# Depthwise-conv taps handed out ahead of the matmuls, and decay work moved later, in a two-layer GLA and conv decoder trunk

## The chip, the cores and the metric

The kernel runs on one core of one Trainium2 chip. The metric is the device time of one execution, in microseconds; lower is better. Three runs of the kernel before gave a median of 1651.48 us, from 1650.69 to 1652.75.

Names used here: PE is TensorE (matmuls), ACT is ScalarE, DVE is VectorE, POOL is GpSimd, SP issues the weight loads. Each engine works through its own queue in program order.

## The reference, cut to what matters

A decoder trunk of two layers. Each layer is a SwiGLU FFN at half weight, a mixer, and a second such FFN, each behind an RMS norm. Tokens: 16 meta tokens and a prompt of 256 (one sequence), and 8 running sequences of 8 new tokens; 336 columns in all, 320 where the meta tokens are no longer wanted. The mixer, where everything of this change lies:

```python
proj = x @ w_in            # q, k, v, g, a_lr, glu (a, ga), m_a, m_b
loga = log_sigmoid(a_lr @ w_decay_up + b_decay) / 16      # per key channel
# gated linear attention in chunks, b = cumsum(loga)
scores = tril((q * exp(b)) @ (k * exp(-b)).T);  o = scores @ v + (q * exp(b)) @ S
S      = exp(b_last) * S + (k * exp(b_last - b)).T @ v
u = a * sigmoid(ga)                                       # conv input
c = silu(rmsnorm(depthwise_conv31(cat(conv_buf, u)) + b_dw))
merged = sigmoid(m_a) * rmsnorm(o) * gla_norm * silu(g) + sigmoid(m_b) * (c @ w_pw)
return merged @ w_out, S, last 30 rows of u per sequence
```

## The kernel before, in words

Activations stand transposed: 128 channels on the partitions, tokens in the columns. All big products are made of three matmuls with fp32r operands (high part by high part, high by low, low by high): `mm3`, L234. A block of 128 output channels takes 8 such triples over the input channels, 24 matmuls.

**Weights.** A plan (`weight_plan`, L67) lists the weight pieces (320 to 512 KB each) in the order of use. SP loads a piece to `raw` (4 buffers), ACT casts it to the high part `wh` (L205), and DVE (FFN and output weights) or POOL (all mixer weights but the last) subtracts to get the remainder `wl` (L207). Taking a piece (`use`, L211) issues the split of the piece three further on.

**The mixer's order** (L343 to L807) is written out by hand; nothing is reordered by a scheduler. On PE: GLU blocks 0 to 2 (each a gate `pga` and a product `pa`; L498), three groups of the value projection `v` (`v_proj`, L474, 72 matmuls each; the first also carries the 16 low-rank decay columns `lr`), GLU blocks 3 to 7, four blocks of queries, four of keys, three gate blocks, and then 21 more gate blocks with the four attention heads spread among them, before the pointwise and output projections. Twice per kernel, once per layer.

**Ticks.** Behind each triple of a projection `tick()` (L228) runs: it takes the next entry of a list of `tasks`, if there is one, and then calls `fill()`. The decay chain is such a list (L535 to L542): low-rank product `decay_z`, absolute value, exponential, logarithm, minimum on DVE, split into `lah` (ACT) and `lal` (POOL), running sums by matmul (`decay_prompt`, `decay_tail`), each at a fixed tick counted from the start of the second value group (24 ticks per value group, 16 per GLU block). So are the heads' steps (L719 to L753): scores and states 21 to 23 ticks into the head before, outputs from tick 0 on; in the last head the rest of the conv is issued at tick 4 (`conv_flush`), its norm's matmul at tick 8.

**The conv.** `conv_gen` (L384) issues the 31 taps of a channel block on DVE, each as a pair (272 prompt columns into bank `acc`, 64 sample columns into `acs`; one bank each, so the next block waits until ACT has copied both out, L401 to L404). `fill()` (L223) decides when a pair is issued, with two clocks of its own: `clock["pe"]` gets n / 2.4 + 2.5 ns for a matmul of n columns (four times that for fp32), `clock["dve"]` n x 1.04 + 110 ns for a DVE instruction (n x 6.25 + 110 for a reciprocal). Both are set to 0 where a mixer begins. One pair may be issued per tick, if `clock["dve"] + 7000 < clock["pe"]`.

**PSUM banks** (`bank`, L161): tag `mm` has four, `aux` two, `cv` and `cs` one each. A new tile of a tag takes the bank of that tag that came free first. A GLU product is evicted by DVE (times `rstd`), and its gate then goes through a sigmoid on ACT; a value group is evicted by ACT alone (L480 to L482).

Of the kernel before, what the change touches and what calls it, by code (L numbers as in the profile page):

```python
# [9 lines left out]
F32 = mybir.dt.float32  # L10
# [19 lines left out]
HEADS = 4  # L30
DK = 128
DV = 256
# [85 lines left out]
def trunk_kernel(ctx, tc, wts, x_in, vecs, consts, masks, wdecay, cache, state,  # L118
                 y_out, sp_out, ss_out, u_out):
    nc = tc.nc  # L120
    PE, ACT, POOL, SP = nc.tensor, nc.scalar, nc.gpsimd, nc.sync
    clock = {"pe": 0.0, "dve": 0.0}
# [6 lines left out]
    def mm(out, a, b, start, stop):  # L129
        n = 1  # L130
        for x in b.shape[1:]:
            n *= x
        clock["pe"] += (n / 2.4 + 2.5) * (4 if b.dtype == F32 else 1)
        PE.matmul(out, a, b, start=start, stop=stop)  # L134
# [26 lines left out]
    def bank(name, tag="mm", bufs=4):  # L161
        return psum.tile([128, 512], F32, tag=tag, name=name, bufs=bufs)
# [4 lines left out]
    def grp(g):  # L167
        return slice(g * 128, (g + 1) * 128)
# [51 lines left out]
    tasks = []  # L220
    filler = [None]

    def fill():  # L223
        if filler[0] is not None and clock["dve"] + 7000.0 < clock["pe"]:
            if next(filler[0], 0) == 0:
                filler[0] = None

    def tick():  # L228
        task = tasks.pop(0) if tasks else None
        if task is not None:  # L230
            task()
        fill()
# [110 lines left out]
    def mixer(l, norm, next_block):  # L343
# [6 lines left out]
        gp = gl.enter_context(tc.tile_pool(name="gla", bufs=1, reuse_waits="tile"))  # L350
# [2 lines left out]
        lal = mp.tile([128, 3, 512], F32R, tag="sb", name="lal")  # L353
        qt = gp.tile([128, HEADS, T], F32, name="qt")
        kt = gp.tile([128, HEADS, TP], F32, name="kt")
        kuT = gp.tile([128, 4, HEADS * DK], F32, name="kuT")
        v = gp.tile([128, 3, HEADS * DV], F32, name="v")
        dec = gp.tile([128, HEADS, 2 * NCH + NS], F32, name="dec")
        rT = gp.tile([128, 3], F32, name="rT")
# [16 lines left out]
        ACT.copy(wds[0:64], wdec[0:64])  # L376
        ACT.copy(wdr[64:128], wdec[64:128])
        POOL.tensor_tensor(out=wds[64:128], in0=wdec[64:128], in1=wdr[64:128].bitcast(F32), op=ALU.subtract)
        POOL.memset(kuT[0:64, 3], 0.0)
        cnorm = Norm()  # L380

        ready = [0]
# [41 lines left out]
        def decay_z(g):  # L424
            pz[g] = bank("pz", *(("aux", 2) if g < 2 else ("mm", 4)))
            mm(pz[g], alr[:, grp(g)], wds, True, True)
            la[g] = kp.tile([128, 512], F32, tag="la", name="la", bufs=3)
            ACT.activation(la[g], pz[g], AF.Abs)
# [9 lines left out]
        def decay_min(g):  # L438
            DVE.scalar_tensor_tensor(out=la[g], in0=pz[g], scalar=0.0, in1=la[g], op0=ALU.min, op1=ALU.subtract)

        def decay_split(g):
            ACT.copy(lah[:, g], la[g])
            POOL.tensor_tensor(out=lal[:, g], in0=la[g], in1=lah[:, g].bitcast(F32), op=ALU.subtract)

        def cumulate(out, hd, g):
            hs = slice(hd * DK, (hd + 1) * DK)
            m = cum[:, 0:2 * CHUNK] if g < NCH else cum[:, 2 * CHUNK:N_CUM]
            mm(out, lah[:, g, hs], m, True, False)
            mm(out, lal[:, g, hs], m, False, True)

        def decay_prompt(hd):
            pb = bank("pb", "aux", 2)
            for g in range(NCH):
                cumulate(pb[:, 2 * g * CHUNK:2 * (g + 1) * CHUNK], hd, g)
            v4 = pb.rearrange("p (g x c) -> p g x c", g=NCH, x=2)
            for dst, x, sign in ((qt, 0, 1.0), (kt, 0, -1.0), (ku, 1, 1.0)):
                ACT.activation(dst[:, hd, 0:SEQ].rearrange("p (g c) -> p g c", g=NCH), v4[:, :, x], AF.Exp,
                               scale=sign / TAU)
            ACT.activation(dec[:, hd, 0:2 * NCH], pb[:, CHUNK - 1::CHUNK], AF.Exp, scale=1.0 / TAU)

        def decay_tail(h0):
            pb = bank("pbt", "aux", 2)
            for e in range(2):
                cumulate(pb[:, 2 * e * TAIL:2 * (e + 1) * TAIL], h0 + e, NCH)
            v4 = pb[:, 0:4 * TAIL].rearrange("p (h x c) -> p h x c", h=2, x=2)
            hh = slice(h0, h0 + 2)
            for dst, x, sign in ((qt, 0, 1.0), (kt, 0, -1.0), (ku, 1, 1.0)):
                ACT.activation(dst[:, hh, SEQ:T], v4[:, :, x], AF.Exp, scale=sign / TAU)
            ACT.activation(dec[:, hh, 2 * NCH:], v4[:, :, 0, LS - 1:NSAMP:LS], AF.Exp, scale=1.0 / TAU)
# [4 lines left out]
        def v_proj(i):  # L474
            nw = V_WIDTH[i]
            nv = nw - (RANK if i == 0 else 0)
            pv = [bank("pv") for _ in range(3)]

            def evict(g):
                if i == 0:  # L480
                    ACT.activation(lr[:, g], pv[g][:, nv:nw], AF.Identity, scale=rT[:, g:g + 1])
                ACT.activation(v[:, g, V_OFF[i]:V_OFF[i] + nv], pv[g][:, :nv], AF.Identity, scale=rT[:, g:g + 1])  # L482

            for c in range(4):
                wh, wl = W.use("v")
                for g in range(3):
                    for k in range(2):
                        kk = 2 * c + k
                        mm(pv[g][:, :nw], xh[:, kk, grp(g)], wh[:, k], kk == 0, False)
                        mm(pv[g][:, :nw], xl[:, kk, grp(g)], wh[:, k], False, False)  # L490
                        mm(pv[g][:, :nw], xh[:, kk, grp(g)], wl[:, k], False, kk == KB - 1)
                        tick()
                    if c == 3:
                        evict(g)
# [36 lines left out]
        for j in range(3):  # L531
            glu_block(j)
        rstd = shared["rstd"]
        v_proj(0)
        at = {0: decay_lr, 12: decay_alr, 32: decay_exp, 36: decay_ln, 102: decay_end}  # L535
        for g in range(3):
            at.update({26 + g: lambda g=g: decay_z(g), 40 + g: lambda g=g: decay_min(g),
                       46 + 3 * g: lambda g=g: decay_split(g)})
        for hd in range(HEADS):
            at[64 + 5 * hd] = lambda hd=hd: decay_prompt(hd)  # L540
        at.update({86: lambda: decay_tail(0), 94: lambda: decay_tail(2)})
        tasks.extend([at.get(k) for k in range(103)])  # L542
        v_proj(1)
        v_proj(2)
        for j in range(3, KB):
            glu_block(j)
# [9 lines left out]
        def transposes(hd):  # L556
            pt = bank("ptr", "aux", 2)
            for g in range(3):
                PE.transpose(pt[:, grp(g)], ku[:, hd, grp(g)], ident)
                clock["pe"] += 108.0  # L560
            hs = slice(hd * DK, (hd + 1) * DK)
            ACT.copy(kuT[:, 0:3, hs], pt[:, :384].rearrange("p (g d) -> p g d", g=3))
            ACT.copy(kuT[64:128, 3, hs], pt[64:128, grp(2)])

        for hd in range(HEADS):
            pk = bank("pk")
# [42 lines left out]
            DVE.copy_predicated(probs[hd % 2].rearrange("p g c -> p (g c)")[:, :n], msk[:, :n], ps[:, :n])  # L609

        def prompt_state(hd, st, part):
            ks = slice(hd * DK, (hd + 1) * DK)
            vs = slice(hd * DV, (hd + 1) * DV)
            pu = bank("upd", "aux", 2)
            if part == 0:
                sp = st["sp"] = hp.tile([128, 2 * NCH, DV], F32, tag="sp", name="sp", bufs=1)
                mm(pu[:, 0:DV], kuT[:, 3, ks], v[:, 2, vs], True, True)
                ACT.activation(sp[:, 0], pu[:, 0:DV], AF.Identity, scale=dec[:, hd, 1:2])
                return
            sp = st["sp"]  # L620
            for g in range(NCH):
                mm(pu[:, g * DV:(g + 1) * DV], kuT[:, g, ks], v[:, g, vs], True, True)
            for g in range(NCH):
                if g:
                    ACT.activation(sp[:, 2 * g], sp[:, 2 * g - 1], AF.Identity, scale=dec[:, hd, 2 * g + 1:2 * g + 2])
                DVE.scalar_tensor_tensor(out=sp[:, 2 * g + 1], in0=sp[:, 2 * g], scalar=dec[:, hd, 2 * g:2 * g + 1],
                                         in1=pu[:, g * DV:(g + 1) * DV], op0=ALU.mult, op1=ALU.add)
            SP.dma_start(sp_out[l, hd], sp[:, 2 * NCH - 1])
# [11 lines left out]

        def mask_ku(hd, st):
            km = st["km"] = hp.tile([64, NS, DK], F32, tag="km", name="km", bufs=1)
            src = kuT[0:64, 2, hd * DK:(hd + 1) * DK]
            POOL.tensor_tensor(out=km, in0=src.unsqueeze(1).to_broadcast([64, NS, DK]),
                               in1=seqm[0:64].unsqueeze(2).to_broadcast([64, NS, DK]), op=ALU.mult)

# [72 lines left out]
        hs = [{} for _ in range(HEADS)]  # L719

        def head_start(hd):
            st = hs[hd]
            return {0: lambda: (scores(hd, st), mask_ku(hd, st)), 1: lambda: prompt_state(hd, st, 0),
                    2: lambda: prompt_state(hd, st, 1)}
# [25 lines left out]
        at = head_start(0)  # L750
# [236 lines left out]
```

## Time and profile before

| | before |
|---|---|
| median of three runs | 1651.48 us (1650.69 to 1652.75) |
| profiled execution, its own time | 1651.98 us |
| its span, first to last instruction | 1650.2 us |
| PE busy | 1617.0 us, 98% |
| DVE busy | 1080.9 us, 66% |
| ACT busy | 734.8 us, 45% |
| POOL busy | 423.6 us, 26% |
| mean granted PE clock | 0.990 |
| HBM read | 230.08 MB, 149 GB/s with the writes |

The busy shares are means over stages; in the mixers (about 253 to 597 us and 1082 to 1406 us) DVE is much busier than 66%. A granted clock of 1 is 2.4 GHz, 0.5 is 1.2 GHz. In a row of the timeline the number in brackets is the time for which the engine had nothing to do just before, with the instruction that ended it. The wait on `acc` by ACT's copy, for example, is time in which DVE could not begin the next conv block.

### The profile page before, as it was taken

The numbers are of one execution on the slowest core, as the hardware profiler recorded it, in microseconds if no ns is written. First come the engines' busy times: TensorE is split into PE (matmuls) and PEld (weight loads), VectorE is DVE, ScalarE is ACT, GpSimd is POOL, SyncE is SP. The second block draws the span as 40 slices with busy tenths as digits, with TensorE's granted clock in tenths as the row PEclk, the third lists the DMA queues.
The fourth block names the chain that finished last, engine by engine and source line by source line (L and its number), as shares of the span: only waits on it lengthen the run. The fifth ranks groups of instructions, "written<-read, shape, count | busy, mean of one in ns | idle before, by whom it ended". The sixth has DMA issues, their size and how long they took to land.

```text
span 1650.2 us, 27122 instructions
## 1 busy us (share of the span) xinstructions
PE 1617.0 (98%) x10612; PEld 1596.8 (97%) x10612; DVE 1080.9 (66%) x2159; ACT 734.8 (45%) x1148; POOL 423.6 (26%) x284
## 2 busy tenths in 40 slices
PE   8999999999999999999999999999999999999997
PEld 7999999999988999999999999999999889999997
DVE  7666446899885466555456564459998865666643
ACT  5433434753445444333333333347644554433432
POOL 0000017675563410000000000076756652000000
PEclk9999999999988999999999999999999999999999
DMA  5654445464452545443445544453644544444352
GB/s 200 200 182 129 133 152 163 134 182 152 129 170 87 166 128 154 145 140 120 147 156 184 174 136 138 151 153 126 193 159 143 169 135 155 146 154 153 116 170 79
DMA packets 76592, 247.56 MB, mean 150 GB/s; under 512 B 8624, under 2 KB 10928, under 8 KB 76208
## 3 DMA queue, kind: packets, MB, share of 16 engines
q1 hardware_dynamic: 75888, 240.34, 46.6%
q10 hardware_dynamic: 576, 5.49, 0.9%
q8 instruction: 83, 1.36, 0.3%
q14 instruction: 45, 0.37, 0.1%
HBM read 230.08 MB, written 15.71 MB: 149 GB/s over the span
## 4 chain that ended last, share of the span: by engine, by line
PE 88%; DVE 6%; ACT 3%; issue 1%; POOL 1%; DMA 0%; SPq 0%; DVEq 0%; POOLq 0%; ACTq 0%
PE pd L134 19%; PE pg L134 19%; PE pu L134 19%; PE pgate L134 5%; PE pga L134 4%; PE pa L134 4%; PE po L134 4%; PE pw L134 3%; PE pv L134 3%; PE pk L134 2%; PE pq L134 2%; PE o L134 2%; DVE acc L112 1%; DVE cl L112 1%; ACT wh L205 1%
## 5 line engine op out<-in xcount | busy, mean ns | idle before, releaser
L112 DVE TENSOR_TENSOR wl<-raw,wh 128x1024 fp32r<-128x1024 f32 (+1 forms) x320 | 349.3, 1108 | 228.0 <-ACT wh L205 227.5
L205 ACT CAST wh<-raw 128x1024 fp32r<-128x1024 f32 (+3 forms) x456 | 428.0, 956 | 77.0 <-issue 27.3
L207 POOL TENSOR_TENSOR wl<-raw,wh 128x1024 fp32r<-128x1024 f32 (+2 forms) x136 | 307.9, 2279 | 141.5 <-ACT wh L205 135.8
L270 POOL TENSOR_TENSOR ssum<-ssum,sq 128x336 f32<-128x336 f32 (+1 forms) x63 | 56.7, 901 | 1018.5 <-ACT sq L269 1018.5
L112 DVE SCALAR_TENSOR_TENSOR acc<-u,vec,acc 128x272 f32<-128x272 f32 (+1 forms) x480 | 234.5, 489 | 0.0
L134 PE MATMUL pg<-xh,wh 128*128 128x336 f32 (+1 forms) x704 | 223.1, 317 | 7.1 <-ACT wh L205 7.1
L134 PE MATMUL pu<-xh,wh 128*128 128x336 f32 (+1 forms) x704 | 221.8, 315 | 0.0
L134 PE MATMUL pg<-xh,wl 128*128 128x336 f32 (+1 forms) x704 | 221.2, 314 | 0.3 <-DVE wl L112 0.3
L134 PE MATMUL pg<-xl,wh 128*128 128x336 f32 (+1 forms) x704 | 221.2, 314 | 0.0
L134 PE MATMUL pu<-xh,wl 128*128 128x336 f32 (+1 forms) x704 | 221.1, 314 | 0.0
L134 PE MATMUL pu<-xl,wh 128*128 128x336 f32 (+1 forms) x704 | 221.1, 314 | 0.0
L134 PE MATMUL pd<-act_hi,wh 128*128 128x336 f32 (+1 forms) x704 | 221.0, 314 | 0.0
L134 PE MATMUL pd<-act_hi,wl 128*128 128x336 f32 (+1 forms) x704 | 220.3, 313 | 0.0
L134 PE MATMUL pd<-act_lo,wh 128*128 128x336 f32 (+1 forms) x704 | 220.2, 313 | 0.0
L134 PEld LDWEIGHTS pg<-xh,wh 128*128 128x128 f32 x704 | 132.6, 188 | 7.4 <-ACT wh L205 7.1
L326 ACT CAST act_hi<-pu 128x336 fp32r<-128x336 f32 (+1 forms) x88 | 38.5, 437 | 217.9 <-DVE pu L112 217.9
L134 PE MATMUL pgate<-xh,wh 128*128 128x336 f32 (+1 forms) x384 | 135.4, 352 | 0.0
L112 DVE SCALAR_TENSOR_TENSOR acs<-u,vec,acs 128x64 f32<-128x64 f32 x480 | 134.7, 281 | 0.0
L134 PEld LDWEIGHTS pg<-xh,wl 128*128 128x128 f32 x704 | 132.5, 188 | 0.8 <-DVE wl L112 0.8
L134 PEld LDWEIGHTS pg<-xl,wh 128*128 128x128 f32 x704 | 132.6, 188 | 0.4
L134 PEld LDWEIGHTS pu<-xh,wh 128*128 128x128 f32 x704 | 132.5, 188 | 0.0
L134 PEld LDWEIGHTS pu<-xh,wl 128*128 128x128 f32 x704 | 132.5, 188 | 0.0
(201 smaller groups left out, 3286.9 us busy)
## 6 DMA issues: line engine op xcount, KB each, us to landing
raw<-in_wts SPq DMA_DIRECT2D x304, 512.0 KB, 3.7
raw<-in_wts SPq DMA_DIRECT2D x64, 384.0 KB, 3.5
raw<-in_wts SPq DMA_DIRECT2D x64, 320.0 KB, 3.0
s<-in_state SPq DMA_DIRECT2D x16, 512.0 KB, 4.5
out_ss<-s SPq DMA_DIRECT2D x16, 512.0 KB, 5.3
raw<-in_wts SPq DMA_DIRECT2D x16, 344.0 KB, 3.6
u<-in_cache ACTq DMA_DIRECT2D x2, 2424.0 KB, 11.7
out_u<-u SPq DMA_DIRECT2D x16, 303.0 KB, 4.7
```

Source lines behind the costliest of these rows:

```text
L112: return fn(*args, **kw)
L134: PE.matmul(out, a, b, start=start, stop=stop)
L205: ACT.copy(wh[:, :nk * nw], raw)
L207: eng.tensor_tensor(out=wl[:, :nk * nw], in0=raw, in1=wh[:, :nk * nw].bitcast(F32), op=ALU.subtract)
L270: eng.tensor_tensor(out=self.sum[:, 0:n], in0=self.sum[:, 0:n], in1=sq[:, 0:n], op=ALU.add)
L326: ACT.copy(ah[:, j, 0:n], pu[:, 0:n])
```

## The change

Three things. `fill()` first lifts DVE's clock to PE's, and then issues pairs in a loop until DVE's clock is 1000 ns ahead of PE's (it leaves the loop if the generator has nothing to issue). The decay tasks are put at later ticks: transposed low-rank columns from tick 12 to 20, `decay_z` from 26 to 44, exponential from 32 to 50, logarithm from 36 to 54, minimum from 40, 41, 42 to 63, 65, 67, splits from 46, 49, 52 to 66, 70, 74, the heads' running sums from 64, 69, 74, 79 to 82, 87, 92, 97, tails from 86 and 94 to 103 and 109, the end from 102 to 118; two of the three tiles of the first value group come from `aux` instead of `mm`. The transposed keys `kuT` are laid out by head, then by group, instead of by group, then by head.

```diff
@@ -221,9 +221,13 @@
     filler = [None]
 
     def fill():
-        if filler[0] is not None and clock["dve"] + 7000.0 < clock["pe"]:
+        clock["dve"] = max(clock["dve"], clock["pe"])
+        while filler[0] is not None and clock["dve"] < clock["pe"] + 1000.0:
+            before = clock["dve"]
             if next(filler[0], 0) == 0:
                 filler[0] = None
+            if clock["dve"] == before:
+                break
@@ -353,7 +357,7 @@
-        kuT = gp.tile([128, 4, HEADS * DK], F32, name="kuT")
+        kuT = gp.tile([128, HEADS, 4, DK], F32, name="kuT")
@@ -376,7 +380,7 @@
-        POOL.memset(kuT[0:64, 3], 0.0)
+        POOL.memset(kuT[0:64, :, 3], 0.0)
@@ -474,7 +478,7 @@
-            pv = [bank("pv") for _ in range(3)]
+            pv = [bank("pv", *(("aux", 2) if i == 0 and g < 2 else ("mm", 4))) for g in range(3)]
@@ -532,14 +536,14 @@
         v_proj(0)
-        at = {0: decay_lr, 12: decay_alr, 32: decay_exp, 36: decay_ln, 102: decay_end}
+        at = {0: decay_lr, 20: decay_alr, 50: decay_exp, 54: decay_ln, 118: decay_end}
         for g in range(3):
-            at.update({26 + g: lambda g=g: decay_z(g), 40 + g: lambda g=g: decay_min(g),
-                       46 + 3 * g: lambda g=g: decay_split(g)})
+            at.update({44 + g: lambda g=g: decay_z(g), 63 + 2 * g: lambda g=g: decay_min(g),
+                       66 + 4 * g: lambda g=g: decay_split(g)})
         for hd in range(HEADS):
-            at[64 + 5 * hd] = lambda hd=hd: decay_prompt(hd)
-        at.update({86: lambda: decay_tail(0), 94: lambda: decay_tail(2)})
-        tasks.extend([at.get(k) for k in range(103)])
+            at[82 + 5 * hd] = lambda hd=hd: decay_prompt(hd)
+        at.update({103: lambda: decay_tail(0), 109: lambda: decay_tail(2)})
+        tasks.extend([at.get(k) for k in range(119)])
@@ -558,9 +562,8 @@
-            hs = slice(hd * DK, (hd + 1) * DK)
-            ACT.copy(kuT[:, 0:3, hs], pt[:, :384].rearrange("p (g d) -> p g d", g=3))
-            ACT.copy(kuT[64:128, 3, hs], pt[64:128, grp(2)])
+            ACT.copy(kuT[:, hd, 0:3], pt[:, :384].rearrange("p (g d) -> p g d", g=3))
+            ACT.copy(kuT[64:128, hd, 3], pt[64:128, grp(2)])
@@ -609,17 +612,16 @@
-                mm(pu[:, 0:DV], kuT[:, 3, ks], v[:, 2, vs], True, True)
+                mm(pu[:, 0:DV], kuT[:, hd, 3], v[:, 2, vs], True, True)
...
-                mm(pu[:, g * DV:(g + 1) * DV], kuT[:, g, ks], v[:, g, vs], True, True)
+                mm(pu[:, g * DV:(g + 1) * DV], kuT[:, hd, g], v[:, g, vs], True, True)
@@ -640,7 +642,7 @@
-            src = kuT[0:64, 2, hd * DK:(hd + 1) * DK]
+            src = kuT[0:64, hd, 2]
```

## Rows read from the trace of the kernel before

**Rows 1.** The page, busy time of each engine (us, share, instructions).

```profile
PE 1617.0 (98%) x10612; PEld 1596.8 (97%) x10612; DVE 1080.9 (66%) x2159; ACT 734.8 (45%) x1148; POOL 423.6 (26%) x284
```

**Rows 2.** Waits of PE: us in total, how many, the longest.

```profile
PE pga L134 <- ACT v L482: 4.0, 2, 2.0
PE pgate L134 <- POOL wl L207: 3.9, 3, 1.6
PE pw L134 <- POOL wl L207: 3.3, 2, 1.7
PE nrm L134 <- POOL ssum L270: 3.2, 2, 2.2
```

**Rows 3.** Stretches of 5 us: busy time of each engine, granted clock, DMA.

```profile
490.00:495.00 5.00, 5.00 (x22) 5.00 (x22) 4.79 (x4) 2.44 (x3) 4.96 (x4) 0.50 0.18 28
...
1310.00:1315.00 5.00, 5.00 (x41) 4.96 (x40) 4.90 (x3) 4.09 (x5) 3.51 (x3) 1.00 0.22 88
```

**Rows 4.** Timeline of PE, conv norm and last head's norm: start, us, instruction, idle before.

```profile
487.09 1.49 PE L134 MATMUL nrm<-ssum,ones_d 128*128 128x336 f32 x2 [2.16 <-POOL ssum L270]
...
510.41 0.73 PE L134 MATMUL nrm<-ssum,ones_v 128*128 128x336 f32 x2
...
1309.40 0.81 PE L134 MATMUL nrm<-ssum,ones_d 128*128 128x320 f32 x2 [1.02 <-POOL ssum L270]
...
1323.05 0.70 PE L134 MATMUL nrm<-ssum,ones_v 128*128 128x320 f32 x2
```

**Rows 5.** Chain that ended last, in order of time: blocks of 24 matmuls.

```profile
266.01 3.68 PE pa L134 x24
...
314.53 5.50 PE pga L134 x24
...
1143.21 3.95 PE pga L134 x24
```

**Rows 6.** Timeline of ACT, first layer, 306 to 324 us.

```profile
306.27 1.67 ACT L432 ACTIVATE la<-la 128x512 f32<-128x512 f32 x3
...
308.90 1.28 ACT L436 ACT_TABLE_LOAD   x1
310.19 1.95 ACT L436 ACTIVATE la<-la,one 128x512 f32<-128x512 f32 x3
312.05 0.35 ACT L401 COPY u<-acc 128x256 f32<-128x256 f32 x1
...
321.67 0.45 ACT L515 ACTIVATE gate<-pga 128x336 f32<-128x336 f32 x1 [2.52 <-DVE pga L112]
322.02 1.99 ACT L205 CAST wh<-raw 128x1024 fp32r<-128x1024 f32 x2
```

**Rows 7.** Timeline of DVE: block 1's gate, and first taps of conv blocks 1 and 2.

```profile
266.22 0.51 DVE L112 TENSOR_TENSOR pga<-pga,rstd 128x336 f32<-128x336 f32 x1
...
288.84 0.56 DVE L112 TENSOR_SCALAR acc<-u,vec 128x272 f32<-128x272 f32 x1 [0.67 <-ACT u L404]
...
312.62 0.56 DVE L112 TENSOR_SCALAR acc<-u,vec 128x272 f32<-128x272 f32 x1 [4.97 <-ACT u L404]
...
1117.48 0.55 DVE L112 TENSOR_SCALAR acc<-u,vec 128x256 f32<-128x256 f32 x1 [0.25 <-ACT u L401]
...
1136.98 0.55 DVE L112 TENSOR_SCALAR acc<-u,vec 128x256 f32<-128x256 f32 x1 [1.21 <-ACT u L401]
```

**Rows 8.** Timeline of POOL, first layer: decay remainders and weight remainders.

```profile
320.06 2.56 POOL L443 TENSOR_TENSOR lal<-la,lah 128x512 fp32r<-128x512 f32 x2
323.14 4.77 POOL L207 TENSOR_TENSOR wl<-raw,wh 128x1024 fp32r<-128x1024 f32 x2 [0.53 <-ACT wh L205]
```

**Rows 9.** Timeline, first layer's last head: state, its use, last conv copy.

```profile
476.50 0.51 ACT L625 ACTIVATE sp<-sp,dec 128x256 f32<-128x256 f32 x1 [0.55 <-DVE sp L112]
...
478.07 0.39 PE L134 MATMUL o<-qt,sp 128*128 128x128 f32 x2
...
484.99 0.37 ACT L401 COPY u<-acc 128x256 f32<-128x256 f32 x1 [2.56 <-DVE acc L112]
```

More of the change, by code (lines that the diff above doesn't have):

```diff
@@ L611, in prompt_state @@
         def prompt_state(hd, st, part):
-            ks = slice(hd * DK, (hd + 1) * DK)
             vs = slice(hd * DV, (hd + 1) * DV)
```

## The prediction

> **What bounds the kernel now.** I read the busy shares first, then what PE (TensorE) waited for, then a table of stretches with the granted clock, then the two places that this shows, row by row. PE is busy for 98% of the span [rows 1], so time can come only from PE's idle gaps and from stretches in which its clock is halved. The list of PE's waits shows where the gaps are [rows 2]: 4.0 us in two pieces of 2.0, one in each layer, for ACT's (ScalarE's) evictions of `v`, 3.2 us for the sum of squares behind the conv norm, 7.2 us for weight remainders from POOL. The table of stretches shows the other loss: from 490 to 495 us, in the first layer, the granted clock is 0.50, that is 1.2 of 2.4 GHz, and in the same stage of the second layer it is 1.00 [rows 3]. So both layers do the same work, one with a slow clock: the second layer is the price list for the first.
>
> The slow stretch, row by row [rows 4]: in the first layer the conv norm's matmul waits 2.16 us (487.09), and up to the last head's norm (510.41) 23.32 us pass; in the second layer the wait is 1.02 us, and the same stretch takes 13.65 us (1309.40 to 1323.05). The difference is 9.67 us; some 45 matmuls there are 336 columns wide in one layer and 320 in the other, 0.3 us, so the half clock costs 9.3 us. The other place is the first gate of GLU block 3 [rows 5]: behind the wait of 2.0 us 24 matmuls take 5.50 us, in the second layer, behind the same wait, 3.95 us, and undisturbed (at 266.01) 3.68 us: another slow stretch, 5.50 - 3.95 = 1.55 us.
>
> **Why PE waits there.** GLU block 3: ACT is in order, and before it may evict the last group of `v` it has the exponentials, a table load of 1.28, the logarithms (1.95 us for three) and conv block 1's copies, which start at 312.05 [rows 6]. DVE (VectorE) meanwhile had finished conv block 1 at 312.62 - 4.97 = 307.65 and stands for those 4.97 us until the copies are done [rows 7]. Conv norm: the last conv block is copied out at 484.99 [rows 9], 2.1 us ahead of the matmul that waits for its squares. DVE has fallen behind because the planner keeps it 7 us back.
>
> **The change, part by part.** *Hand-out of taps.* By the planner's formulas a tap pair costs 393 + 177 = 570 ns, three matmuls 427.5 ns; on the chip the 31 pairs of conv block 1 take 18.81 us, 0.61 us each (288.84 to 307.65; 18.29 us and 0.59 in the second layer) [rows 7], and three matmuls 3.68 / 8 = 0.46 us [rows 5]. Both are 1.04 to 1.08 times the planner's, so the planner's lead or lag holds on the chip. After GLU block 0 the clocks stand at 48 x 0.1425 + 0.6 = 7.4 us (PE) and 2.3 + 1.6 = 3.9 us (DVE: reciprocals, products). Before, no pair is handed out until PE is 7 us ahead; after, DVE's clock is set to PE's and pairs are issued up to 1 us ahead. Carrying both clocks through the program gives the pairs that stand ahead of each eviction: block 1's gate 0 before and 8 after, block 2's second product 15 and 22, block 3's gate 73 and 83 (second layer 75 and 86), the last head's scores 235 and 240 (237 and 243), of 248. No DVE work is added or taken away; evictions get 4 to 6 us more of it in front of them. DVE reaches block 1's gate at 266.22 before [rows 7], and would at 266.22 + 8 x 0.61 = 271.1 after; PE is done with it at 266.01 [rows 5], so the lag is 5 us. Up to the end of conv block 1 DVE's queue holds the same work, so that it ends at 307.65 in both.
>
> *Other banks for the first value group.* PE ends GLU block 2 and begins the value projection at 266.01 + 3 x 3.68 = 277.05; with that lag block 2's last product leaves its bank at about 282. Two tiles in the `aux` banks and one in block 1's bank (free at about 272) are there in time and cost nothing; three tiles in `mm` would have made PE wait for it, some 3 us.
>
> *Exponentials behind the value projection.* Same instructions and as many table loads, 16 to 18 ticks later (the transposes 8). ACT now stands at conv block 1's copies until 307.65 (a wait hidden by weights that are split three pieces ahead), then does copies and square (about 1.0), three casts (1.0 each [rows 6]), and is at the evictions of `v` at about 311.7. PE ends the projection at 314.53 - 2.0 = 312.5. So the two waits of 2.0 us go, and with the first its slow stretch of 1.55: -5.6 us.
>
> What is late next: the running sums of the first head, at tick 82. PE reaches them 35 triples after 312.5, at 312.5 + 35 x 0.46 = 328.6. They need both remainders `lal` of groups 0 and 1, which POOL makes behind two weight remainders, the first of which needs a cast that ACT issues behind block 3's sigmoid. DVE comes to block 3's gate 21 pairs after 307.65: 307.65 + 0.4 + 21 x 0.61 = 320.9, done 321.3. ACT has, from 307.65, some 1.0 + 4 x 1.0 + 3.0 (three evictions and three absolute values, taken as the sigmoid's 0.45 to 0.5 each) + 1.28 + 1.67 + 1.28 + 1.95 = 14.2 us of work, to 321.9, then table load and sigmoid 1.73 [rows 6]. So the cast ends between 322.8 (DVE alone) and 324.6 (ACT in full). POOL then has 4.77 + 2.56 = 7.33 us [rows 8]: 330.1 to 331.9, against 328.6. A new wait of 1.5 to 3.3 us; I take 2.7, nearer to ACT's chain because ACT is in order. In the second layer DVE ends block 1 at 1136.98 - 1.21 = 1135.77 [rows 7], 24 pairs follow, and PE ends the projection at 1143.21 - 2.0 = 1141.2: the same sums give 2.1 and 2.7, and I take 2.4. Together +5.1 us. The clock fell after one of two waits of 2 us there; I count one slow stretch: +1.55 us.
>
> *The end of the conv.* At the last scores 5 pairs fewer are left (3.0 us), in the second layer 6 (3.5 us), while the waits were 2.16 and 1.02 us. DVE's lag at this point should be near that of before: its extra pairs (7 x 0.61 = 4.3 us) are paid by the 4.97 us in which it no longer stands, and PE is earlier by only 2.0 + 1.55 - 2.7 = 0.9 us. So both waits go, -3.2 us, and the clock stays up: -9.3 us. What comes late behind it is the weight remainders: with PE back at full clock POOL, ACT and DVE have 9.3 us less there to prepare them. The five such waits of both layers sum to 7.2 us, none over 1.7 [rows 2]; another one in the first layer costs 0 to 1.7, and I take 1.0, between the two.
>
> *Keys by head.* Same copies, same sizes; the waits list has no PE wait on `kuT` [rows 2]. POOL's memset has the same elements. Zero; no PE wait on the masked keys stands there either, so what POOL does with them has cover.
>
> **Sum**: -5.6 + 5.1 + 1.55 - 3.2 - 9.3 + 1.0 = -10.5 us against the profiled execution's 1651.98 us (span 1650.2): **1641.5 us**. That execution is 0.5 us over the median of three.
>
> **A rule against it.** In the rows the clock is halved right behind the wait of 2.16 us, and not behind one of 2.0 us in the second layer [rows 4, 5]. So a wait of this size is enough in one place and not in another, and whether it is the cause is a reading. The Trainium skill, page "TensorE: Matmul & The Clock Gate", section on HAM oscillation, warns only of longer idle gaps than these; by it the waits would not be the cause, the clock would fall all the same, and the sum would be 9.3 us higher. The first layer's trace speaks against it, the fall being at the wait itself.
>
> **Rivals.**
> - *No wait at tick 82*: ACT and POOL get through sooner than I add up, or the lag is smaller. For it: my chain adds seven durations, and 2 us off each would do. Against: DVE's path alone is late by 1.5. Time: 1641.5 - 5.1 - 1.55 = 1634.9.
> - *The clock falls in the first layer's head stage anyway*, with or without a wait: many short matmuls lie there, and a wait of 2.0 us did not halve the clock in the second layer [rows 5]. Against: the fall is right at the wait [rows 4], and the second layer's same stage keeps 1.00 [rows 3]. Time: 1641.5 + 9.3 = 1650.8, no change.
> - *Slower: the head stage waits for DVE.* The state `sp` is ready at 476.50 + 0.51 = 477.01 and used at 478.07 [rows 9]: 1.06 us of slack. If DVE's lag there grows by more (it would if its 4 us were not paid back, for example by new waits at ACT's copies), PE waits some 4.3 - 1.06 = 3.3 us in each layer and the clock halves in both: 1641.5 + 6.6 + 2 x 9.3 = 1667. Against: the payback above; it decides from a lag of 1.1 us more than before.
>
> **Chances.** Forecast 0.52 (1640 to 1647: no or both slow stretches, waits of 1.5 to 3.3 us, a remainder of the conv wait); no wait 0.26; clock falls anyway 0.11; slower 0.11. Three runs of before spread over 2 us, so 0.2% (3.3 us) is about what can be told from no change. Faster 0.78, same 0.11, slower 0.11. The range takes in the first two cases with their bounds, from 1633 to 1648; the other two, 0.22, are left out but for their near edge.
>
> **What would show it.** Right: no PE wait on `v` at GLU block 3; a wait of PE on POOL's `lal` or on weight remainders in GLU block 5; no wait of the norm on `ssum`; clock 1.00 in the stretch that was at 0.50; DVE without its 4.97 us. Wrong: a PE wait on ACT's `sp` or on `probs`, a granted clock under 0.9 in either head stage, or GLU evictions that hold a bank so long that PE waits for DVE.

## The result, and the profile after

The changed kernel took 1641.28 us, the median of four executions (1639.13 to 1642.78), against 1651.15 for the kernel before beside it: a ratio of 0.9945, interval [0.9929, 0.9961], 0.55% faster. The forecast was 1641.5. The profiled execution took 1640.1 us (span 1638.3, mean granted clock 0.997). Ratios and ranges in this document compare fast executions only and leave out two that were far off, one of 6316.68 us of the kernel before and one of 2166.25 us (mean clock 0.747) of the last variant below.

The page after, busy time of each engine, answers to [rows 1]: DVE, ACT and POOL do the same work, PE is busy for 8.6 us less.

```profile
PE 1608.4 (98%) x10612; PEld 1588.8 (97%) x10612; DVE 1081.3 (66%) x2159; ACT 732.8 (45%) x1148; POOL 422.8 (26%) x284
```

What PE waited for after (us in total, how many, the longest), to be laid beside [rows 2]; a wait of 6.8 us for the first weights, 7.1 before, is not shown:

```profile
PE pgate L134 <- POOL wl L207: 4.3, 4, 1.6
PE pb L134 <- POOL lal L447: 3.4, 4, 1.3
PE pw L134 <- POOL wl L207: 3.3, 2, 1.7
PE upds L134 <- DVE s L112: 1.0, 1, 1.0
...
PE nrm L134 <- POOL ssum L274: 0.2, 1, 0.2
```

The two waits on `v` are gone, the conv norm's 3.2 us are 0.2, the late remainders cost 7.6 instead of 7.2, and there are new waits: 3.4 us on `lal`, and one of 1.0 us for DVE's update of the sample states `s`.

The clock after, stretches of 5 us (busy time of PE, PEld, DVE, ACT, POOL, granted clock, DMA share, GB/s): the first layer's last head runs at 1.00 where it ran at 0.50 [rows 3], and a short new loss stands in the second layer's head 1.

```profile
490.00:495.00 5.00, 5.00 (x31) 3.68 (x30) 4.96 (x10) 4.02 (x7) 1.61 (x3) 1.00 0.30 102
...
1255.00:1260.00 5.00, 3.95 (x20) 2.89 (x19) 5.00 (x13) 2.28 (x6) 2.74 (x5) 0.87 0.31 107
1260.00:1265.00 5.00, 5.00 (x27) 4.84 (x27) 3.22 (x11) 1.12 (x2) 5.00 (x4) 0.78 0.11 12
```

PE's timeline after: two of the sums' waits, the norms of [rows 4], and the new wait in head 1 of the second layer.

```profile
328.46 0.28 PE L134 MATMUL pb<-cum,lah 128*128 128x256 f32 x1
330.03 0.38 PE L134 MATMUL pb<-cum,lal 128*128 128x256 f32 x1 [1.29 <-POOL lal L447]
...
331.26 0.39 PE L134 MATMUL pb<-cum,lal 128*128 128x256 f32 x1 [0.72 <-POOL lal L447]
...
480.69 0.73 PE L134 MATMUL nrm<-ssum,ones_v 128*128 128x336 f32 x2
...
483.84 0.83 PE L134 MATMUL nrm<-ssum,ones_d 128*128 128x336 f32 x2 [0.15 <-POOL ssum L274]
...
497.06 0.73 PE L134 MATMUL nrm<-ssum,ones_v 128*128 128x336 f32 x2
...
1256.92 1.91 PE L134 MATMUL upds<-v,km 32*128 32x256 f32 x8 [0.96 <-DVE s L112]
...
1298.26 0.70 PE L134 MATMUL nrm<-ssum,ones_d 128*128 128x320 f32 x2
...
1311.15 0.70 PE L134 MATMUL nrm<-ssum,ones_v 128*128 128x320 f32 x2
```

These landmarks and those of [rows 4] split the gain by place. Up to the first layer's conv norm, 487.09 to 483.84: -3.25 us. From there to the last head's norm, 23.32 to 13.22 us: -10.10. From there to the second layer's conv norm the lead over the kernel before shrinks from 13.35 to 11.14 us: +2.21. Second layer, conv norm to last head's norm, 13.65 to 12.89: -0.76. Together -11.90, all of the difference of the spans (1650.2 to 1638.3).

The rows of the other engines after are to be laid beside [rows 6 to 9]. First ACT's timeline:

```profile
307.30 0.37 ACT L405 COPY u<-acc 128x256 f32<-128x256 f32 x1 [5.70 <-DVE acc L112]
...
313.42 0.57 ACT L486 ACTIVATE v<-pv,rT 128x344 f32<-128x344 f32 x1
...
322.49 0.45 ACT L519 ACTIVATE gate<-pga 128x336 f32<-128x336 f32 x1
322.84 1.99 ACT L205 CAST wh<-raw 128x1024 fp32r<-128x1024 f32 x2
...
480.37 0.38 ACT L405 COPY u<-acc 128x256 f32<-128x256 f32 x1
```

DVE's timeline, the gates of blocks 1 and 3 and the first tap of conv block 2:

```profile
271.15 0.51 DVE L112 TENSOR_TENSOR pga<-pga,rstd 128x336 f32<-128x336 f32 x1
...
307.90 0.56 DVE L112 TENSOR_SCALAR acc<-u,vec 128x272 f32<-128x272 f32 x1 [0.44 <-ACT u L408]
...
320.63 0.50 DVE L112 TENSOR_TENSOR pga<-pga,rstd 128x336 f32<-128x336 f32 x1
```

POOL's timeline, weight and decay remainders:

```profile
323.95 4.80 POOL L207 TENSOR_TENSOR wl<-raw,wh 128x1024 fp32r<-128x1024 f32 x2 [5.04 <-ACT wh L205]
328.72 2.49 POOL L447 TENSOR_TENSOR lal<-la,lah 128x512 fp32r<-128x512 f32 x2
```

DVE comes to block 1's gate at 271.15 (worked out: 271.1) and to block 3's at 320.63 (320.9), and its stand of 4.97 us is 0.44. ACT now waits ahead of conv block 1's copy, 5.70 us, and PE has no wait there.

### The profile page after: what moved, and what is told of

The parts are those of the page before. It is cut to its first block, busy times and chain, and to the rows that moved or that the text cites. A ratio compares the mean times of both kernels' runs of the same rounds, so it can differ in the third digit from the quotient of the medians.

```text
span 1638.3 us, 27112 instructions
## 1 busy us (share of the span) xinstructions
PE 1608.4 (98%) x10612; PEld 1588.8 (97%) x10612; DVE 1081.3 (66%) x2159; ACT 732.8 (45%) x1148; POOL 422.8 (26%) x284
## 4 chain that ended last, share of the span: by engine, by line
PE 85%; DVE 10%; ACT 2%; issue 1%; POOL 1%; DMA 0%; SPq 0%; DVEq 0%; POOLq 0%; ACTq 0%
PE pd L134 19%; PE pg L134 19%; PE pu L134 19%; PE pgate L134 6%; PE po L134 4%; PE pw L134 4%; DVE acc L112 3%; PE pa L134 2%; PE pga L134 2%; PE pk L134 2%; PE o L134 2%; PE pq L134 2%; PE pv L134 1%; DVE acs L112 1%; DVE cl L112 1%
## 5 line engine op out<-in xcount | busy, mean ns | idle before, releaser
L134 PEld LDWEIGHTS pu<-xl,wh 128*128 128x128 f32 x704 | 132.6, 188 | 0.0
```

## The experiments

Each time is the median of 5 to 12 executions. In its executions beside the first four runs the kernel before itself ranged from 1646.09 us (mean granted clock 0.994) to 1654.54 (0.988).

**Hand-out and banks alone.** The kernel before with the new `fill()`, and:

```diff
-            pv = [bank("pv") for _ in range(3)]
+            pv = [bank("pv", *(("aux", 2) if i == 0 and g < 2 else ("mm", 4))) for g in range(3)]
```

> The kernel before with the new hand-out of taps and the new banks of the first value group; the decay tasks stay at their old ticks, the keys in their old layout. Theory A (the gain comes from the decay tasks, because DVE no longer stands for 5 us at conv block 1 and so the conv ends sooner; the early hand-out only moves DVE work about): the two waits of PE on `v` stay, about 2 us each, DVE still stands for about 5 us behind conv block 1, the last conv copy comes within 1 us of 485.0, the conv norm still waits about 2 us in the first layer and its head stage runs at 0.50: 1651, within 2 us of the kernel before. Rival B (the hand-out ahead is what ends the conv sooner): the last conv copy 3 to 5 us earlier, no conv norm wait, clock 1.00 there: 1651.5 - 3.2 - 9.3 + 1 = 1640, with the `v` waits still in the list.

Measured: 1651.63 us, ratio 1.0016 [1.0004, 1.0028], no gain. But the place is the rival's: the conv norm waits 0.15 us, and the last head takes 13.21 us to its norm. The gain is given back at GLU block 3. PE's timeline of this run:

```profile
319.16 0.65 PE L134 MATMUL pga<-xh,wh 128*128 128x336 f32 x1 [5.29 <-DVE la L112]
...
1141.29 0.65 PE L134 MATMUL pga<-xh,wh 128*128 128x336 f32 x1 [5.86 <-ACT v L486]
```

ACT's timeline of it, conv block 1's copy and the exponentials:

```profile
308.64 0.37 ACT L405 COPY u<-acc 128x256 f32<-128x256 f32 x1 [3.93 <-DVE acc L112]
...
312.45 1.67 ACT L436 ACTIVATE la<-la 128x512 f32<-128x512 f32 x3
```

With taps handed out earlier, conv block 1's copies are issued ahead of the exponentials; ACT stands 3.93 us for DVE there, the exponentials start at 312.45 instead of 306.27 [rows 6], and the waits of 2.0 us become 5.3 and 5.9, with half clock behind them in both layers.

**Decay ticks alone.** The kernel before with this part of the diff alone:

```diff
-        at = {0: decay_lr, 12: decay_alr, 32: decay_exp, 36: decay_ln, 102: decay_end}
+        at = {0: decay_lr, 20: decay_alr, 50: decay_exp, 54: decay_ln, 118: decay_end}
...
-        tasks.extend([at.get(k) for k in range(103)])
+        tasks.extend([at.get(k) for k in range(119)])
```

> The kernel before with the new ticks of the decay tasks alone; hand-out of taps, banks and keys as before. Theory A: no wait of PE on `v`, DVE's stand behind conv block 1 under 1 us, last conv copy near 480.4, no conv norm wait over 0.5 us, first layer's head stage at 1.00. GLU evictions have 4 to 6 us less DVE work ahead of them than in the changed kernel, so the weight remainders and `lal` come earlier and the wait at the running sums is 0 to 3.4 us: 1638 to 1642. Rival B: the conv norm wait and the half clock stay, the `v` waits with their slow stretch go: 1651.5 - 5.6 + 0 to 3 = 1646 to 1649.

Measured: 1650.43 us, ratio 1.0003 [0.9990, 1.0015]. No wait on `v`, 0.44 us of stand behind conv block 1, `lal` 2.7 us: as theory A has it. But the conv norm waits as before. ACT's timeline of this run, the last conv copy:

```profile
483.44 0.37 ACT L401 COPY u<-acc 128x256 f32<-128x256 f32 x1 [2.56 <-DVE acc L112]
```

PE's timeline of it, third head's norm and the two conv norms:

```profile
480.38 0.73 PE L134 MATMUL nrm<-ssum,ones_v 128*128 128x336 f32 x2
...
485.54 0.86 PE L134 MATMUL nrm<-ssum,ones_d 128*128 128x336 f32 x2 [2.16 <-POOL ssum L270]
...
1304.83 0.90 PE L134 MATMUL nrm<-ssum,ones_d 128*128 128x320 f32 x2 [1.02 <-POOL ssum L270]
```

The last conv copy stands 3.06 us behind the third head's norm (483.44 - 480.38), exactly as before (484.99 - 481.93), although DVE no longer loses 4.97 us at conv block 1. DVE's timeline of this run shows most of that loss again, in GLU blocks 3 to 5:

```profile
322.68 0.64 DVE L112 TENSOR_TENSOR u<-pa,gate 128x16 f32<-128x16 f32 x3 [1.19 <-ACT gate L515]
...
333.70 0.52 DVE L112 TENSOR_TENSOR pga<-pga,rstd 128x336 f32<-128x336 f32 x1 [1.00 <-PE pga L134]
...
338.36 0.56 DVE L112 TENSOR_SCALAR acc<-u,vec 128x272 f32<-128x272 f32 x1 [3.55 <-ACT u L404]
```

The stand at conv block 2's copies was 0.44 us before (336.81). And in the heads DVE waits for PE in both kernels, so a lead from the GLU blocks is not carried through them: for `upds` between 400 us and the last conv copy 2.6 us before, 1.8 us here. After the change the copy stands 0.32 us ahead of the third head's norm (480.37 - 480.69). That is 3.4 us better, and the 5 pairs of 0.61 us that no longer stand between make up 3.05 of it. So neither part gains alone; together they gain 10 us.

**Only the last pairs moved.** The run above, with a smaller lag from the first head on:

```diff
-        if filler[0] is not None and clock["dve"] + 7000.0 < clock["pe"]:
+        if filler[0] is not None and clock["dve"] + lag[0] < clock["pe"]:
...
+        lag[0] = 4000.0
         at = head_start(0)
```

> The kernel before with the new decay ticks, the old banks and keys, and the old hand-out up to the first head; from there the lag that the planner keeps is 4000 ns instead of 7000. It asks which part of the new hand-out ends the conv norm's wait. Theory (it is the 5 or so pairs that no longer stand ahead of the last conv copy, wherever they were issued): by the planner 240 pairs stand ahead of the last scores (235 before, 240 in the changed kernel), the last conv copy comes right with the third head's norm instead of 3.06 us behind it, no wait on the sum of squares, granted clock 1.00 in the first layer's last head; no waits on `v`, `lal` 2.7 us as in the run with the new ticks alone: 1641.3 - 0.7 = 1640.6, or 1637.5 if the wait for DVE in the second layer's head 1 and its slow stretch also go. Rival (the lead has to be built up early, since DVE is behind by then): wait of about 2 us and half clock as with the ticks alone, 1650.

Measured: 1646.19 us, 1643.01 to 1657.84, ratio 0.9991 [0.9972, 1.0011]; the time of the theory, 1640.6, was missed. Most of its mechanism is there: 240 pairs ahead of the last scores, the last copy 0.37 us behind the third head's norm, no conv norm wait in the second layer, the last head at 1.00. Of the first layer's wait 0.84 us are left, PE's timeline:

```profile
487.36 0.83 PE L134 MATMUL nrm<-ssum,ones_d 128*128 128x336 f32 x2 [0.84 <-POOL ssum L271]
```

But DVE has the pairs to do in the heads now: PE waits 2.6 us for `s` instead of 1.0, and the clock falls behind two of these waits in the profiled execution (0.94 us at 444.02, 1.40 us at 1261.21). Four of the twelve executions took 1652.06 to 1657.84 us at a mean clock of 0.992 or less; none of these was profiled. Here a lead built up early did better than one built up in the heads.

**Conv norm later.** The kernel before with:

```diff
-                at.update({4: conv_flush, 8: conv_norm_a, 12: conv_norm_b, 23: lambda: head_norm_a(hd, st),
+                at.update({4: conv_flush, 12: conv_norm_a, 23: lambda: head_norm_a(hd, st),
...
-                    at[k] = lambda b=b: conv_scale(b)
+                    at[k] = lambda b=b: (conv_scale(b) if b else (conv_norm_b(), conv_scale(0)))
```

> The kernel before with the conv norm's matmul four ticks later (tick 12 instead of 8) and its inverse two ticks later, all else as before. It asks whether the wait makes the clock fall. Theory (the wait of 2.16 us is the cause): no wait of PE on the sum of squares in either layer, first layer's head stage at 1.00, 1651.5 - 3.2 - 9.3 + 0 to 2 (scales 2 ticks later, weight remainders) = 1639 to 1641. Rival (the clock falls there anyway): 0.50 in that stage all the same, 1651.5 - 3.2 = 1648.

Measured: 1647.72 us, ratio 0.9987 [0.9976, 0.9998]. No wait at the norm, yet the clock falls a little later in both layers, behind waits that were not there before (first layer) or were shorter (second layer, 0.37 us for `s`); PE's timeline:

```profile
493.08 1.97 PE L134 MATMUL upds<-v,km 32*128 32x256 f32 x6 [0.50 <-ACT sd L285]
...
1314.46 2.32 PE L134 MATMUL upds<-v,km 32*128 32x256 f32 x8 [1.65 <-DVE s L112]
```

By itself this run does not decide between the wait and "the clock falls anyway"; the time is the rival's.

**Conv norm earlier.** The changed kernel with the wait put back; run twice.

```diff
-                at.update({4: conv_flush, 8: conv_norm_a, 12: conv_norm_b, 23: lambda: head_norm_a(hd, st),
+                at.update({4: conv_flush, 6: conv_norm_a, 12: conv_norm_b, 23: lambda: head_norm_a(hd, st),
```

> The changed kernel with the conv norm's matmul two ticks earlier (6 instead of 8). It puts a wait of about 2 us back in the first layer's last head and asks what it does to the clock there. Two triples and a head's first sample outputs, 0.9 + 1.1 us, no longer stand ahead of it: wait 0.15 + 2.0 = 2.1 us; in the second layer about 0 to 1 us. Theory (the wait lets the clock fall): granted clock at 0.50 behind it, for up to the 9.3 us that it cost before: 1641.3 + 2.0 + 5 to 9 = 1648 to 1653. Rival (the wait is harmless, the clock falls for another reason): 1641.3 + 2 = 1643, granted clock 1.00 there.

> The kernel with the conv norm two ticks earlier, unaltered, profiled again. Its first profile had the wait of 1.93 us at the norm and a granted clock of 1.00 behind it, at 1645.18 us, while 7 of its 12 executions took 1650.7 to 1659.1. It asks whether those are executions in which the clock falls at that wait. Theory: the wait is 1.9 us again, and a profiled execution above 1650 shows 0.50 behind it for 5 to 20 us; one below 1646 shows 1.00 there. Rival: an execution above 1650 shows 1.00 there and 0.50 somewhere else.

Measured, first run: 1650.88 us, but as two heaps: five executions from 1642.66 to 1645.18 (mean clock 0.996 or 0.997) and seven from 1650.72 to 1659.13 (0.993 or less). The second run of the same kernel: five from 1643.30 to 1645.31 and three from 1651.86 to 1652.51. The profile of the first is of the lower heap (1645.18 us), that of the second of the upper (1652.08). The first run, a window of 5 us:

```profile
490.00:495.00 5.00, 5.00 (x40) 4.54 (x38) 4.86 (x4) 2.89 (x4) 2.91 (x2) 1.00 0.02 5
```

Its PE timeline, conv norm and last head's norm:

```profile
485.58 0.83 PE L134 MATMUL nrm<-ssum,ones_d 128*128 128x336 f32 x2 [1.93 <-POOL ssum L274]
...
500.81 0.72 PE L134 MATMUL nrm<-ssum,ones_v 128*128 128x336 f32 x2
```

The second run, the same window:

```profile
490.00:495.00 5.00, 5.00 (x24) 5.00 (x23) 4.86 (x4) 2.93 (x4) 2.87 (x2) 0.50 0.01 2
```

Its PE timeline, the same two norms:

```profile
485.18 0.91 PE L134 MATMUL nrm<-ssum,ones_d 128*128 128x336 f32 x2 [1.93 <-POOL ssum L274]
...
509.20 0.73 PE L134 MATMUL nrm<-ssum,ones_v 128*128 128x336 f32 x2
```

One program, one wait of 1.93 us: from it to the last head's norm 15.23 us at 1.00 in one execution, and 24.02 us in the other, about 20 of them at 0.50. The wait makes the fall possible, not certain. Over all profiles but that of the later norm (whose two stages fell behind the other waits shown), of the 18 last-head stages whose norm waits 0.16 us or less (at its old tick or the earlier one) none lost its clock; of the eight whose norm waits 0.67 to 2.16 us four did.

**The changed kernel again,** unaltered.

> The changed kernel again, unaltered, beside the next two. It asks how much of the spread between executions is left where no wait stands in the last head's stage. Theory (a wait there lets the clock fall in some executions and not in others): the kernel before spread over 8.5 us and the run with the conv norm two ticks earlier over 16.5 us; this one stays within 4 us, median 1640 to 1642.5, mean granted clock 0.996 or more in nearly all. Rival (the spread belongs to the chip): executions at 1648 to 1653 here as well, with a mean clock near 0.990.

Measured: 1641.88 us, 1639.41 to 1642.05, ratio 0.9948 [0.9928, 0.9967]; mean clock 0.996 or 0.997 throughout. With a wait of only 0.16 us in the last head the upper heap is gone. What spread is left fits two small places, the waits on `lal` and the one for `s`: in this profile (1642.05 us) the clock also falls behind the waits on `lal` in the first layer (0.81 from 330 to 335 us), which it did not in the first profile of this kernel.

**Old banks.** The changed kernel with:

```diff
-            pv = [bank("pv", *(("aux", 2) if i == 0 and g < 2 else ("mm", 4))) for g in range(3)]
+            pv = [bank("pv") for _ in range(3)]
```

> The changed kernel with the old banks (all three tiles of the first value group from the four banks that the GLU blocks use). Theory (the prediction's): GLU evictions stand behind 8 to 22 tap pairs more, so PE waits for DVE's last product of block 2 at the start of the value projection, about 3 us in each layer: 1641.3 + 6 = 1647, and 1650 if the clock falls behind the waits. Rival: a bank is free in time after all, no wait there, 1641.

Measured: 1642.18 us, ratio 0.9946 [0.9934, 0.9958]: nothing. PE's waits in this run:

```profile
PE pb L134 <- POOL lal L447: 2.8, 4, 0.7
...
PE pv L134 <- ACT gate L519: 0.9, 2, 0.7
...
PE pv L134 <- ACT v L486: 0.3, 1, 0.3
```

There is a wait, 1.2 us and not 6. Of it 0.9 us are for block 2's gate, which frees the last bank that is needed, not its product, and 0.3 us for an eviction of `v`. And PE, later by that, waits 0.6 us less for `lal`.

**Old layout of the keys,** on the changed kernel; its copies, memset, state matmuls and masked keys follow:

```diff
-        kuT = gp.tile([128, HEADS, 4, DK], F32, name="kuT")
+        kuT = gp.tile([128, 4, HEADS * DK], F32, name="kuT")
```

> The changed kernel with the transposed keys in their old layout. Theory (the prediction's): nothing waits for these copies, 0: 1641, within 1.5 us of the changed kernel run beside it. Rival: the copies, the state matmuls or the masked keys read the old layout more slowly, 1643 or more.

Measured: 1640.60 us, ratio 0.9947 [0.9930, 0.9965]; the same. This run is also the two halves above together, without the keys.

**All sums six ticks later,** on the changed kernel; the end goes to 124:

```diff
-            at[82 + 5 * hd] = lambda hd=hd: decay_prompt(hd)
-        at.update({103: lambda: decay_tail(0), 109: lambda: decay_tail(2)})
+            at[88 + 5 * hd] = lambda hd=hd: decay_prompt(hd)
+        at.update({109: lambda: decay_tail(0), 115: lambda: decay_tail(2)})
```

> The changed kernel with the running sums, tails and end of the decay chain six ticks later (88 to 103, 109, 115, 124). It asks whether the wait on `lal`, 3.4 us in both layers, is paid for in the end or only a hand-over of the same lag. Theory: PE arrives 6 x 0.46 = 2.8 us later at the first sum, which covers the 1.29 + 0.72 and the 0.64 + 0.73 us: no wait on `lal`, 1641.3 - 3.4 = 1637.9, or up to 1 us more where the weight remainders then come later. Rival: the exponentials behind the sums now crowd ACT ahead of the queries or the transposed keys, or POOL's weight remainders take the wait over in full: 1641, no gain.

Measured: 1644.47 us, ratio 0.9968 [0.9957, 0.9980], 3 us slower than the changed kernel (nine executions from 1642.60 to 1645.99 us, against ten from 1639.13 to 1642.78). The waits on `lal` are gone, but PE waits 2.68 and 2.93 us for the third head's banks. ACT's timeline:

```profile
336.29 0.45 ACT L519 ACTIVATE gate<-pga 128x336 f32<-128x336 f32 x1 [3.32 <-DVE pga L112]
...
338.99 0.38 ACT L461 ACTIVATE qt<-pb 128x256 f32<-128x256 f32 x1
```

Six ticks put the first exponentials behind block 5's sigmoid, where ACT stands 3.32 us for DVE; after the change they start at 333.67, ahead of it.

**Only the first head's sums later,** on the changed kernel.

```diff
-            at[82 + 5 * hd] = lambda hd=hd: decay_prompt(hd)
+            at[82 + 5 * hd if hd else 86] = lambda hd=hd: decay_prompt(hd)
```

> The changed kernel with the first head's running sums four ticks later (86 instead of 82), so that two heads' sums follow each other and the order of exponentials and sigmoids on ACT stays. Theory: PE arrives 4 x 0.46 = 1.84 us later, so 0.2 of the 2.0 us wait on `lal` is left in the first layer and none of the 1.4 us in the second: 1641.3 - 3.2 = 1638.1. Rival: as with all sums six ticks later, PE waits for ACT's exponentials to free the banks of the sums, 1 to 3 us in each layer: 1640 to 1644.

Measured: 1637.03 us, ratio 0.9924 [0.9912, 0.9937], the size of the theory. `lal` costs 0.7 us instead of 3.4, ACT's exponentials 1.2.

**And the second sample states at tick 20,** on top of that:

```diff
-                18: lambda: sample_state(hd, st, 1),
+                20 if hd + 1 < HEADS else 18: lambda: sample_state(hd, st, 1),
```

> The changed kernel with the first head's running sums at tick 86 (as in the run before) and the second half of the sample states at tick 20 instead of 18 in all heads but the last. Two ticks are 0.92 us, the wait of PE for DVE in the second layer's head 1 is 0.96 us. Theory: that wait goes and none comes in its place; 1637.0 - 1.0 = 1636.0, and no execution above 1640, as the clock has no wait to fall behind in the heads. Rival: the next head's state now waits for its bank, since DVE updates the samples' states just ahead of it: 1637 to 1640.

Measured: 1635.98 us, ratio 0.9915 [0.9896, 0.9934]; the executions compared lie from 1635.34 to 1637.10. The wait for `s` falls from 1.0 to 0.3 us, a conv norm wait of 0.67 and one of 0.5 us on a head's copy come in. So the theory's "none comes in its place" was wrong, and its time right. It is the fastest version run, 15 us under the kernel before, though its interval and that of the run above overlap.

## Why the prediction was right, and where its steps were not

**The total** was right, and mostly for its reasons. By the places of the split above, the forecast's terms give: up to the first conv norm -2.0 - 1.55 + 2.7 - 2.16 = -3.0 (measured -3.25); first layer's last head -9.3 (-10.10); from there to the second layer's conv norm +1.0 - 2.0 + 2.4 + 1.55 - 1.02 = +1.9 (+2.21); second layer's last head 0 (-0.76). That the median came within 0.2 us of the forecast is luck: profile against profile 11.9 us went, where 10.5 were forecast, and the single terms were off both ways. The 0.2% that was to be told from no change rested on three runs 2 us apart and was too narrow a base. The 74 executions of the kernel before that were compared in the experiments range from 1646.01 to 1654.65 us, at a mean clock of 0.994 to 0.988. The ten of the changed kernel, 1639.13 to 1642.78 us at 0.996 to 0.998, still lie clear of them all.

**"Its extra pairs are paid by the 4.97 us in which it no longer stands"** is the step that failed, though its number held. The ticks alone took that stand away and left the conv norm's wait at 2.16 us; the hand-out alone left ACT and DVE standing for each other and took the wait away. DVE carries neither debt nor lead from GLU block 3 into the last head: with the ticks alone it stood again in blocks 3 to 5, and in the heads it waits for PE with or without the 4.97 us. What ended the wait is the first half of the same step, the 5 pairs that no longer stand between the last scores and the last copy. The slower rival, which hung on that debt, falls with it: nothing more of it was seen than the 0.96 us for `s`. That wait did set off one of the prediction's signs of being wrong, a granted clock under 0.9 in a head stage: 0.87 and 0.78 in the second layer's head 1, from 1255 to 1265 us.

**The wait at tick 82**, +5.1 us forecast, was 3.4: 2.0 and 1.4 for 2.7 and 2.4. POOL's end was right (the second remainder is taken at 331.26, worked out 330.1 to 331.9), but I counted PE as idle from 328.46 to there. It does matmuls with `lah` and the first `lal` in between, and the end of ACT's cast, 323.9 by POOL's start, lay between my two bounds.

**The slow stretch** of 1.55 us was put behind that wait and came, in the profiled execution, behind another: the 0.96 us for `s` in the second layer's head 1 (in the second profile of the changed kernel it came behind both). The forecast had no term for that wait. It belongs to the hand-out: eight pairs more stand ahead by then (220 instead of 212), and the wait is in the run with the hand-out alone too (0.97 us).

**The half clock**, -9.3 us: the size was 10.1, as the stretch takes 13.22 us and not the 14.0 that were taken over from the second layer (13.65, and 0.3 for the wider matmuls). It is the price in the profiled execution: the fastest of the kernel before, at 1646.01 us and a mean clock of 0.994, fits a shorter slow stretch, but none of those was profiled. The reading that the wait causes it is borne out by the earlier norm, in a weaker form: with it the clock may fall, and without it it fell in none of 18 stages. That also says what the second layer's 1.00 in the profile of before was worth as a price list: right for the price, but not a property of that layer. In the run with the ticks alone the second layer has its wait of 1.02 us and falls to 0.50 as well (21.82 us to the last head's norm). The rule weighed against this step, of the Trainium skill, page "TensorE: Matmul & The Clock Gate", section on HAM oscillation, names longer gaps; these rows differ from it, with falls behind waits of 0.5 to 2.16 us among the heads' short matmuls.

**The banks**, 3 us a layer had they stayed, were worth 1.2 us in both layers together, and nothing in the time: of the four banks the one of block 2's last product was not among the three needed. **Keys by head** at zero held.

## What to carry to other kernels

When two stages share an in-order engine, moving work in one can be worth nothing until the other moves too: here each half of the change alone read as no change, and the profile of each half, not its time, showed the gain and where it was given back. Where small waits let the clock fall in some executions only, judge an edit by many executions, and price such a wait by the whole slow stretch that may follow it. To shift a step, count what it passes in the other engines' order: four ticks for the first head's sums gained 4 us, where six for all sums lost 3.

## What the runs showed of the hardware

The clock's fall behind a short wait differs from one execution of a program to the next: 1.93 us at the same matmul, once 1.00 and once 0.50 for about 20 us. Place seems to matter as well: the waits of 1.5 to 1.7 us for late remainders, in the gate blocks behind the heads, kept 1.00 in every profile, while one of 0.50 us in the heads did not. The waits of the sums six ticks later did both: 2.93 us in the second layer kept 1.00, behind 2.68 us in the first the clock was 0.69 from 340 to 350 us. The 0.96 us for `s` also went both ways: half clock behind it in the changed kernel's profile, none in that with the old banks. What decides it in one execution stays open; no run here took that apart.
